# Another order of steps, weight loads and splits in a hybrid attention block on one Trainium2 core

## The chip, the cores and the metric

The kernel runs on one core of one Trainium2 chip, in one launch. The metric is device time in microseconds (us), lower is better; the inputs lie in HBM in a layout made ahead of the launch. The engines are TensorE (PE, matrix products; PEld is its weight load), VectorE (DVE), ScalarE (ACT), GpSimd (POOL) and SyncE (SP, which here issues nearly all DMAs). Each runs its own instructions in the order in which the program wrote them, and waits where one of them needs another engine's result.

## The reference

One block on `x` (512 tokens, width 1024): a norm, one wide input projection, four mixers of 512 columns each, an output projection with a residual, and a final norm. Float32 throughout.

```python
h = rmsnorm(x, norm_g)
p_fox, p_ssm, p_nsa, p_mem = split(h @ w_in)
mem_kv = rmsnorm(mem, mem_norm_g) @ w_mem_kv
# fox: 8 heads of 64: causal softmax attention, scores + c[q] - c[k] with c = cumsum(log_sigmoid(f + bias)); * silu(gate)
# ssm: causal conv of 4 taps, silu, state-space recurrence in chunks of 128, gated by silu(z), group norm
# nsa: 8 query heads on 2 key heads: attention to compressed blocks + chosen blocks + window, with a distance bias
#      (512 tokens: every block is chosen); three gates; * silu(gate)
# mem: 4 heads of 128, softmax attention to 256 memory tokens; * silu(gate)
x = x + concat(o_fox, o_ssm, o_nsa, o_mem) @ w_out
out = rmsnorm(x, final_norm_g)
```

## The kernel before

**Tiles and splits.** TensorE multiplies in a reduced form (`fp32r`). To hold float32 accuracy every operand is split in a rounded part and a remainder, and a product is three: high x high, low x high, high x low. The normed activations are `hh` and `hl` (high and low), eight 128x512 pieces of each. The weights come as 75 tiles of 128x1024 in one array, in the order of the table `ORDER`. A tile is named by what it projects and its number: `fq`, `fk`, `fg` are queries, keys and gate of fox; `xb`, `z` the convolution's input and the gate of ssm; `nq`, `ng`, `ks`, `kw`, `kc`, `vc` queries, gate, selected, window and compressed keys and values of nsa; `mq`, `mk`, `mv`, `mg` those of mem; `bv`, `bc` columns wanted first; `wo0` to `wo3` the output projection of the four mixers.

Each tile passes three steps. `load` issues its DMA on SyncE into one of three buffers `raw`. `split` rounds it on ScalarE to `wh` and subtracts, on VectorE or GpSimd, to `wl`; there are three buffers of `wh` and `wl` too, and a `raw` buffer is free after the subtraction. Then TensorE runs the tile's products: 24 of 128x512 into a PSUM tile `pj`, which other engines read off. What reads `pj` depends on the kind of tile: for `fq` into `L` and `M` (each with an upper and a lower half), for `fk` into `Rk` and `Rl`, for `kc`, `vc` into `kv` and on into `xst` and `xp`.

**Mixers.** Five pipes (fox, ssm, nsa, mem, cmp for the compression; a sixth prepares the distance bias) take their blocks through stages. In fox, stage 0 multiplies `L`, `M` with `Rk`, `Rl` into `pS`, takes the softmax (`pF`, with `nm` the negative maximum, `sm` the sum, `rs` its reciprocal), later stages transpose through DRAM (`fl` to `far` to `pt`, on SyncE's queue), and stage 3 multiplies with the values into `pO`. In ssm `m`, `ce`, `yc`, `xde`, `sq` are masks with exponentials, decayed inputs, outputs and squares; `rmr` is the mean-square root of the memory's norm. In nsa `ct` is a transposed tile of probabilities of the compressed blocks.

**What sets the order.** The engines' programs are written out by one pass over the string `PLAN`, two characters for each step. `L0` issues the next load, `W0` splits the next tile, `.n` runs n pieces of the projection in hand (a piece is three products, or the evacuation of the finished tile), a letter `f`, `s`, `n`, `m`, `c` or `p` with a digit runs that stage of that pipe for its next block, `O` splits the output of a mixer and `B` takes a step of the memory's norm. Since `PLAN` has `W` steps, the scheduler follows it strictly (`follow`), and a tile that is needed and not yet split is split then (`get`). The third table, `PICKS`, gives for each name of a tile a string of letters: which engine does the first, the second, the third copy or subtraction with this name (A ScalarE, V VectorE, P GpSimd). `pick` reads it. No timing model takes part in what follows the front of the program. The opening, up to the tile `fq0`, is written by code of its own.

All instructions are recorded by one helper, so that every row of the profile has its line, L360; tiles are told apart by name.

Of the kernel before, what the change touches and what calls it, by code (L numbers as in the profile page):

```python
# [16 lines left out]
S, D, M = 512, 1024, 256  # L17
# [34 lines left out]

ORDER = (
# [9 lines left out]
)  # L63
KEYS_A = [k for k in ORDER if k[0] not in ("bv", "bc", "mv") and k[0][:2] != "wo"]


PLAN = (
    "p0.9W0.8L0.5W0.2L0p1W0.7L0L0.2W0.9L0L0.6W0.6W0f0f0f0.6L0L0.3f1.6W0.1W0.5f0L0.4f1.6W0f1.3L0f1L0.6W0.3"
    "f2.5L0.1f3.1f0f2f0f0f2.3W0W0f2.4f3f1.2f1.4f2f2f4.5f3.1f3W0f0f4f0L0.6f4.2f5.1f1L0.3f3.1W0L0.4W0f4f1f0"
    "f2f0f1.6L0L0.5f3f3.6W0W0f0.2f1f1f2.1f2.2f4f4.1W0f3f3s0.1f4f1f4f0f0f0f1f1f1f4f2f2.2f3.5L0L0.4f5f2f2.1"  # L70
    "f2f3f2.4W0W0.6f4L0L0f0L0f3c0.1W0.3f5.1f3f5f5f5f3.5W0.9.1f4f4f5.4f4f4O0f1f5f5L0.1s0s0.3L0f2s1s1.5W0.2"
    "f5W0.2f5f5f3f3s2f5c1f4f5s3f4f5B0f5O0c2O0W0.1O0s1.9.3s0L0W0.3s2s2c3s3L0s3.2L0L0.5s4s1.9.2W0W0.3s2L0s5"
    "W0s3B0B0B0.2L0.3s4L0s4s4.1B0.1W0.9.6W0W0s5s5s5n0n0.7L0.2L0n1.3W0W0.2L0L0L0n0n1n0.1n1.3n2n2n2.8n1W0n3"
    "n0.1n1W0.5n2W0L0n3n4n4n2.4n0n0n3n5n5n3L0.8n1n1W0L0n4n0.2O1O1.2n2.3n3.3n2.2W0.1n3n0.1n0n0n1n1.3O1.3L0"
    ".1L0.3n2W0W0n5.2n1n1n0n0n4n4n4.4L0.1n2W0O1.7n1n1n3n4n2n2n3n3n2n0L0.2n3n3n0n5.5W0n5n3n2.4L0.1n5n3n0n4"
    "n4.1n5n5.4n0n1n4n4n0L0n1n1W0n2n0n2n4.3n1.1n2.3n5L0.4W0.3n5.4n2W0n5n5.3n1n1n3n0n0n0.8L0L0.1n3W0n2n1n1"
    ".4n3n3n3.3n1n4n4n4n4.1W0n5n2W0n5n5n5n0n0n0n0.3n1.1n4.1n2n2.1n2.2L0n3.3W0.9n3.1n1n3.2B0n4n4.2n0L0L0n2"
    ".3L0n4.1n4n1W0n1n2n5n5n3.1W0.2n5.3n0n0n3n1n3.8n2.1n0.3n0W0L0L0n2.5n2n1n5n1n4n4n4n3n1W0n3n3n0n2.2n2n1"
    "n4n4.1n3.3n4W0.9n2.3L0m0m0L0m0.2W0L0.3W0.2n1m1n5m1n5n5n5n4m1n2.2n5n5O2n5n3n3m2.1n2W0.4m2.1m3.1m2.1m3"
    "m3m4n4m0m0m0m0n5m4m4n3n5.1n3.1m5m5O2m1m1n4.1n4m2L0n4n5n5m2L0m1m3m6n5L0m2m5O2O2m3m3m0.2m4.1W0.4m4.5W0"  # L80
    "m4.3m5m5m5m1m1m2W0m6m6m2m3m3.1L0.1L0.3m4m4L0.2m6.4W0.4m6m6.1m5m5.1W0.2m6m6.2W0.9.9.9.9.1"
)


PICKS = {
    "M": "VAAAVVVA",
    "Rk": "AVVAAVVV",
    "Rl": "VAAAAAVA",
    "ce": "PPVVVV",
    "ct": "AVAAVAVVAAVAVVVA",  # L90
    "kh0": "AVV",
    "kh1": "AVV",
    "ll": "PVPVPPVV",
    "m": "PVVPVPVV",
    "ml": "PVPV",
    "ol": "VVPVPPVPVPPVPPV",
    "pF": "VVVVVVVAVAVVVVAVAAVVVVVAAVVVAVVV",
    "pM": "VAAVVVAAVAVVVAVA",
    "pN": "AVVVAAVVAVAAAAVAVAVAVAAAVVVVVAAVAAVAVVAAAVVVAVAVAAAVAVVAVVAAVVVV",
    "sq": "VPVPVPPV",  # L100
    "wl": "PVPPPPPPPPPPVVVPVPVPPVVVPPPVPPVVPVVPVPPVPVPPVVPVPPVPPPPVVPPPPPVPVPVPPPVV",
    "xde": "VVV",
    "xp": "VVPVVVVV",
    "yc": "PVVVVVVVVVVPVVVP",
}


# [2044 lines left out]
```

## Time and profile before

| | |
|---|---|
| time, median of 3 runs | 511.45 us (511.14 to 514.05) |
| the profiled execution | 511.3 us, its span 509.5 us, mean granted clock 0.997 |
| busy in the span: PE, DVE, ACT, POOL | 97%, 72%, 58%, 32% |
| weight tiles loaded / split | 75 of 512 KB each |
| bytes moved by DMA | 92.66 MB, mean 182 GB/s |

TensorE is busy nearly all the time and is what the other engines feed. "Busy" counts a row from its start to its modelled end, and rows of TensorE overlap, so a gap shown is a little shorter than the time lost. "Idle before, releaser" in the profile names what ended a wait. The front of the program, to about 42 us, loads and projects `bv` and `bc`; then come fox with the first tiles of ssm and of the compression (to about 180 us), ssm with the output projection of fox (to about 260), nsa (to about 440) and mem with the last tiles of the output projection.

### The profile page before, as it was taken

The page shows a single profiled execution, that of the slowest core. Times are in us where ns is not written, and L with a number is a line of the kernel's source. Part 1 is how long each engine was busy: PE and PEld are TensorE (multiplying, and loading weights), DVE is VectorE, ACT ScalarE, POOL GpSimd, SP SyncE. Part 2 cuts the span into 40 slices and gives each one's busy share as a digit, 9 for nine tenths or more (in the row PEclk, how much of TensorE's full clock was granted, in tenths as well). Part 3 has the DMA queues.
Part 4 walks back from the last instruction along what each step waited for, and adds up shares of the span by engine and source line. Part 5 has one row for each costly group of instructions (what it writes and reads, how often), then busy time and mean ns, then how long its engine had stood idle before and what let it go on. Part 6 is the DMA issues. An engine that isn't in the chain of part 4 may idle for free.

```text
span 509.5 us, 8995 instructions
## 1 busy us (share of the span) xinstructions
PE 496.4 (97%) x2965; PEld 419.6 (82%) x2965; DVE 368.9 (72%) x981; ACT 297.3 (58%) x671; POOL 164.4 (32%) x113
## 2 busy tenths in 40 slices
PE   8999999989999999999899999999999999999995
PEld 5898877877788888888788888788888898898884
DVE  5486686667678688997988786787777786655644
ACT  5856366777545535664464776755756654664343
POOL 3594303030133103643653132340251220521532
PEclk9999999999999999999999999999999999999998
DMA  8791824526687679444345477777766776832213
GB/s 300 314 326 53 93 85 144 183 79 170 155 262 214 194 228 373 130 171 170 132 152 172 123 225 198 238 219 213 197 196 212 233 233 163 255 138 83 84 41 124
DMA packets 72446, 92.66 MB, mean 182 GB/s; under 512 B 26784, under 2 KB 50624, under 8 KB 72400
## 3 DMA queue, kind: packets, MB, share of 16 engines
q1 hardware_dynamic: 71968, 91.51, 58.5%
q10 hardware_dynamic: 432, 0.59, 0.3%
q8 instruction: 23, 0.38, 0.3%
q14 instruction: 23, 0.19, 0.1%
HBM read 73.68 MB, written 20.55 MB: 185 GB/s over the span
## 4 chain that ended last, share of the span: by engine, by line
PE 56%; DVE 19%; ACT 9%; DMA 6%; issue 5%; SPq 2%; POOL 2%; POOLq 0%; ACTq 0%; DVEq 0%
PE pj L360 25%; PE po L360 10%; PE pb L360 7%; PE pO L360 5%; PE pS L360 4%; ACT pN L360 3%; DMA raw<-in_wst 3%; DVE wl L360 2%; DVE fl L360 2%; SPq L360 2%; DVE pN L360 1%; DVE xs L360 1%; ACT pF L360 1%; DMA far<-fl 1%; DVE rs L360 1%
## 5 line engine op out<-in xcount | busy, mean ns | idle before, releaser
L360 POOL TENSOR_TENSOR wl<-raw,wh 128x1024 fp32r<-128x1024 f32 (+1 forms) x44 | 109.3, 2493 | 258.9 <-ACT wh L360 182.9
L360 PE MATMUL pj<-hh,wl 128*128 128x512 f32 x352 | 137.6, 391 | 3.5 <-POOL wl L360 2.8
L360 PE MATMUL pj<-hh,wh 128*128 128x512 f32 x352 | 138.5, 393 | 0.5 <-ACT wh L360 0.5
L360 PE MATMUL pj<-hl,wh 128*128 128x512 f32 x352 | 137.2, 390 | 0.0
L360 PEld LDWEIGHTS pj<-hh,wl 128*128 128x128 f32 x352 | 66.1, 188 | 19.1 <-POOL wl L360 3.6
L360 ACT ACTIVATE wh<-raw 128x1024 fp32r<-128x1024 f32 (+1 forms) x72 | 73.3, 1034 | 8.5 <-DMA raw<-in_wst 3.4
L360 PEld LDWEIGHTS pj<-hh,wh 128*128 128x128 f32 x352 | 66.1, 188 | 14.7 <-ACT wh L360 0.9
L360 PEld LDWEIGHTS pj<-hl,wh 128*128 128x128 f32 x352 | 66.1, 188 | 13.0
L360 ACT ACTIVATE pN<-pN,nm 128x128 f32<-128x128 f32 (+7 forms) x96 | 45.3, 473 | 37.5 <-DVE nm L360 36.3
L360 DVE TENSOR_TENSOR wl<-raw,wh 128x1024 fp32r<-128x1024 f32 (+1 forms) x29 | 37.8, 1310 | 4.6 <-ACT wh L360 4.1
L360 PE MATMUL po<-wh,oh 128*128 128x512 f32 x96 | 37.7, 393 | 0.0
L360 PE MATMUL po<-wh,ol 128*128 128x512 f32 x96 | 37.5, 390 | 0.0
L360 PE MATMUL po<-wl,oh 128*128 128x512 f32 x96 | 37.5, 390 | 0.0
L360 ACT ACTIVATE pF<-pF,nm 128x128 f32<-128x128 f32 (+3 forms) x32 | 17.8, 556 | 28.3 <-DVE nm L360 27.4
L360 DVE TENSOR_TENSOR acc<-acc,po 128x512 f32<-128x512 f32 (+1 forms) x33 | 21.1, 663 | 9.9 <-PE po L360 9.8
L360 DVE STREAM_TRANSPOSE fl<-pN 128x128 f32<-128x128 f32 (+3 forms) x64 | 27.9, 482 | 0.1
L360 DVE SCALAR_TENSOR_TENSOR rs<-sm,gat 128x3 f32<-128x3 f32 x32 | 6.6, 206 | 28.8 <-ACT pN L360 28.8
L360 ACT ACTIVATE pN<-pN,rs 128x128 f32<-128x128 f32 (+3 forms) x31 | 16.1, 544 | 12.9 <-DVE rs L360 12.9
L360 DVE CUSTOM_DVE_ANT_0 pN<-pS,bt 128x128 f32<-128x128 f32 (+5 forms) x80 | 22.1, 320 | 0.1
L360 DVE SCALAR_TENSOR_TENSOR xs<-x,cwh,xs 128x512 f32<-128x512 f32 x24 | 19.0, 790 | 4.0 <-ACT xs L360 3.4
L360 PEld LDWEIGHTS po<-wh,ol 128*128 128x128 f32 x96 | 18.0, 188 | 3.8
L360 PEld LDWEIGHTS po<-wl,oh 128*128 128x128 f32 x96 | 18.0, 188 | 3.6
(273 smaller groups left out, 1009.2 us busy)
## 6 DMA issues: line engine op xcount, KB each, us to landing
raw<-in_wst SPq DMA_DIRECT2D x73, 512.0 KB, 5.0
far<-fl SPq DMA_DIRECT2D x144, 64.0 KB, 2.1
pt<-far SPq DMA_DIRECT2D x36, 256.0 KB, 3.9
far<-fl SPq DMA_DIRECT2D x96, 48.0 KB, 1.7
pt<-far SPq DMA_DIRECT2D x24, 192.0 KB, 2.9
rows<-rv SPq DMA_DIRECT2D x4, 656.0 KB, 7.1
bt<-rows SPq DMA_DIRECT2D x4, 528.0 KB, 4.9
xn<-in_xn SPq DMA_DIRECT2D x4, 512.0 KB, 7.2
```

The source lines that it names most:

```text
L360: return f(*a, **k)
```

## The change

`ORDER`, `PLAN` and `PICKS` are replaced by others; nothing else is. Pools, stages, the number of buffers and the arithmetic of every step are the same.

```diff
 ORDER = (
     ("bv", 0), ("bv", 1), ("bv", 2), ("bv", 3), ("bc", 0), ("bc", 1), ("bc", 2), ("fq", 0), ("xb", 6),
-    ("fk", 1), ("xb", 3), ("xb", 0), ("fk", 0), ("kc", 0), ("fk", 3), ("fk", 2), ("fq", 1), ("fq", 3),
-    ("fq", 2), ("fg", 0), ("vc", 0), ("xb", 1), ("z", 2), ("xb", 5), ("fg", 2), ("z", 3), ("xb", 7), ("fg", 3),
+    ("fk", 1), ("xb", 3), ("xb", 0), ("fk", 0), ("kc", 0), ("fk", 3), ("fq", 2), ("fq", 1), ("fq", 3),
+    ("fg", 0), ("vc", 0), ("xb", 1), ("fk", 2), ("xb", 5), ("fg", 3), ("z", 2), ("fg", 2), ("xb", 7),
...
-    ("ks", 0), ("nq", 2), ("mv", 0), ("mv", 1), ("mv", 2), ("mv", 3), ("nq", 1), ("mg", 3), ("wo0", 2),
...
+    ("wo0", 1), ("nq", 2), ("ks", 0), ("mv", 0), ("mv", 1), ("mv", 2), ("mv", 3), ("nq", 1), ("mg", 3),
...
 PLAN = (
-    "p0.9W0.8L0.5W0.2L0p1W0.7L0L0.2W0.9L0L0.6W0.6W0f0f0f0.6L0L0.3f1.6W0.1W0.5f0L0.4f1.6W0f1.3L0f1L0.6W0.3"
...
+    "L0L0.9.1W0.1p0.5W0.4L0.4L0.5W0.2L0.9W0.5W0.9p1f0f0.5L0.9W0W0L0f1.4W0.7L0L0.5f1f0.3W0.1f0f1f1.2L0f2.1"
...
 PICKS = {
-    "Rk": "AVVAAVVV",
-    "Rl": "VAAAAAVA",
+    "Rk": "VVAAAAAV",
+    "Rl": "VAAVVVAA",
...
-    "pF": "VVVVVVVAVAVVVVAVAAVVVVVAAVVVAVVV",
+    "pF": "AAVAVVVAAAVVVVVVAAVAVVAAVAAAAVVA",
...
-    "wl": "PVPPPPPPPPPPVVVPVPVPPVVVPPPVPPVVPVVPVPPVPVPPVVPVPPVPPPPVVPPPPPVPVPVPPPVV",
+    "wl": "PVPPPPPPPPPPPPVPPVPVPVVPPPPVPPVPPVPVPVVPPVPPVPVPPPPPPPPPPVPPPPVPPPVVPPVP",
...
```

`PLAN` has 690 steps instead of 694: as many loads but one (63), as many splits (64) and stages, and the same pieces of projection (582) in 171 steps instead of 175. In `PICKS`, GpSimd subtracts 52 weight remainders of 72 instead of 44; ScalarE scales 16 of 32 fox probabilities (`pF`) instead of 8; five `Rk` copies instead of three and four `Rl` copies instead of six are ScalarE's; three of the `xp` sums more and one `xde` are GpSimd's. The front of each engine's program and its end stay as they were.

Three places follow, as the engines' programs have them, one row for each instruction or run of like instructions: operation, what is written, what is read, the size. First ScalarE in the fox stretch, before the change. The first `wh` is the split of `fq3`, the second that of `fq2`, the `L` and `M` rows read off `fq1`, and the last `wh` is the split of the gate tile `fg0`.

```order
L360 CAST Rk<-pj 64x512
L360 ACTIVATE wh<-raw 128x1024
L360 ACTIVATE Rk<-pj 64x512 x2
L360 CAST Rl<-cr 64x512
L360 ACTIVATE wh<-raw 128x1024
L360 ACTIVATE pF,sm<-pF,nm 128x512 x2
L360 ACTIVATE pF<-pF,rs 128x512
L360 ACTIVATE L<-pj 64x512 x2
L360 CAST M<-L 64x512
L360 ACTIVATE M<-cst 64x512
L360 CAST M<-L 64x512
L360 ACTIVATE wh<-raw 128x1024
```

The same place after the change; the first row of `wh` are the splits of `fq1` and `fq3`, the first `L` and `M` rows read off `fq2`, and the single `wh` is that of `fg0`.

```order
L360 ACTIVATE Rk<-pj 64x512 x2
L360 CAST Rk<-pj 64x512 x2
L360 ACTIVATE wh<-raw 128x1024 x2
L360 ACTIVATE L<-pj 64x512 x2
L360 ACTIVATE M<-cst 64x512
L360 CAST M<-L 64x512
L360 ACTIVATE M<-cst 64x512
L360 ACTIVATE wh<-raw 128x1024
L360 ACTIVATE L<-pj 64x512 x2
L360 CAST M<-L 64x512
```

The three query tiles ahead of `fg0` are `fq1`, `fq3`, `fq2` before and `fq2`, `fq1`, `fq3` after; in both its split follows the evacuation of the first of them. Before, the softmax rows of 512 (`pF`) stand ahead of that evacuation, after they don't, and more attention products lie between the split and its use. The evacuation of the key tile `fk2` (the second group of `Rk`) has left this place.

Second GpSimd, as a difference, from the root of the memory's norm (`rmr`) to the compression's sums (`xp`).

```order
 L360 TENSOR_TENSOR wl<-raw,wh 128x1024
 L360 TENSOR_TENSOR rmr<-rmv,nhalf 128x2
-L360 TENSOR_TENSOR wl<-raw,wh 128x1024 x11
+L360 TENSOR_TENSOR wl<-raw,wh 128x1024 x16
 L360 MEMSET xp 128x16x2
 L360 TENSOR_TENSOR xp<-xst,x_89 128x8x31
 L360 MEMSET xp 128x16x2
+L360 TENSOR_TENSOR xp<-xst,x_89 128x8x31 x3
```

Five more subtractions stand in this run, and three more sums come behind it.

Third ScalarE in the ssm stretch, ahead of nsa's first query tiles. Before, where the three `wh` are `ks0`, `nq2` and `mv0`:

```order
L360 ACTIVATE sq<-yc 128x512 x2
L360 ACTIVATE L<-pj 64x512 x2
L360 ACTIVATE ce<-m 128x512 x2
L360 ACTIVATE m<-m,nacs 128x128 x8
L360 ACTIVATE wh<-raw 128x1024 x3
L360 ACTIVATE sq<-yc 128x512
```

After, where they are `nq2`, `ks0` and `mv0`:

```order
L360 ACTIVATE sq<-yc 128x512
L360 ACTIVATE ce<-m 128x512 x2
L360 ACTIVATE m<-m,nacs 128x128 x8
L360 ACTIVATE L<-pj 64x512 x2
L360 ACTIVATE wh<-raw 128x1024 x3
L360 ACTIVATE sq<-yc 128x512 x2
```

The exponentials of the ssm chunk (`ce`, `m`) have moved ahead of the evacuation `L` of the query tile before; the three splits stand behind both as before, and more of TensorE's work lies between the first of them and its use.

More of the change, by code (lines that the diff above doesn't have):

```diff
@@ L67 @@
 PLAN = (
-    "p0.9W0.8L0.5W0.2L0p1W0.7L0L0.2W0.9L0L0.6W0.6W0f0f0f0.6L0L0.3f1.6W0.1W0.5f0L0.4f1.6W0f1.3L0f1L0.6W0.3"
[L69 to L81, printed above, removed]
+    "L0L0.9.1W0.1p0.5W0.4L0.4L0.5W0.2L0.9W0.5W0.9p1f0f0.5L0.9W0W0L0f1.4W0.7L0L0.5f1f0.3W0.1f0f1f1.2L0f2.1"
@@ new lines @@
+    "L0.1W0.9.2f0f2f2f0f2.3W0W0.3L0f0.7f1f1L0f1.6W0f3.2f3.2L0.3f4W0f2f4.1f0f1.5W0.3f3f3f3f2f2f3.8f0f0L0f0"
+    "L0L0.2f2.1f3.6f1.4W0.4L0f1.1f1W0W0f2f0s0f3f3.2f4f0f0f4f4f4f1f4f2f2f2f4f0f1f1f1.4f4.1W0f3.1L0.5L0.2W0"
+    "f3f0.2L0f2f3f2f5.5f3f4f4B0f1f5f5f5f5.1W0.1f5.6L0.8c0s0W0f4f5.9.2f2f5W0f5f2f5s1s1f5f3f5.5f4f4L0L0W0.1"
+    "f3.3f5.1f3L0W0s2c1s3L0O0s0f4f4c2f5f5f5s1.9s0.5O0O0O0.2s2W0s2c3s3s1s4L0.9s2W0.7L0L0.3s5.1W0W0s3s3B0B0"
+    ".1B0.4B0.2s4s4s4.9W0.1L0.6L0.2s5s5W0W0s5n0L0n0L0.6W0.5W0n1n0n1L0n0n1.1L0.2L0.1n2n2.2W0n2.5W0.3n1n0n1"
@@ new lines @@
+    ".1L0.7n3n3W0L0.1n2n0n4n0n3n2.4n3.1L0.2n4O1.2n1n1W0n0n5.4O1O1.4n4.3W0.2n1n2n3n3W0n0n0n0.9.1L0.2n2W0n1"
+    "n2n1n1n3n4n4L0n4n0n0n4n2n2.3n3.5n2n3n3O1.4n5n5n5W0.1n1n1L0n0n0.4n3.1W0n5n5.3L0L0.1n2n2n0n3W0n4n4.1L0"
+    ".6n1n1n1n2n3n0n0n0.9W0.2n2n5.2n1n1n1n4L0n4n4n2n5n5.2n0n3W0n0.2L0.6n2.3n3.4W0.1n0n1.1n2n3.1W0.4L0W0n4"
+    "n4n4n4n1n3n5n2n5L0n1n2n2n0n5n0.1n0n0n4.2n5n2n1.1n5.1n5.1n3n3n3n3.9n5W0.1n4n5.2n1.2L0.4L0n4.4n1n4n1.4"
+    "W0W0n0n2n0n0.6n3n3L0n2n1.1n2.2n3n4B0.4n1n3.3n0.1n2L0W0.2n0n2n2.2n4n4n4n1n4n5n1W0n0.3n3n3.2n1L0L0.5n3"
@@ L82 @@
+    ".7W0.1m0n4m0m0n5n5n5n4n4W0.1n2n2n2.6n1n5m1m1m2m3L0L0n5n5n5m1.3W0.3n3.1n5.1n5.1m2m2W0.1m0m4m3m5O2n5m3"
+    "m4m4m0m0m5m0m5n2.1n3n3n3.2m1m1n4n4n5n4n4n5n5n5O2O2L0O2W0m2m1m1m0.2m2m2m3m3m2.2m4m4.1m3.5L0L0L0m4.2W0"
+    "m1W0W0m3L0L0m5m5m2.2m3.1m6.1m6.3m6.1m6.3W0.1m4.1W0.2m4.5m5m5m6m6m5m6m6.9.9.9.9.5"
 )
 PICKS = {
-    "M": "VAAAVVVA",
-    "Rk": "AVVAAVVV",
-    "Rl": "VAAAAAVA",
[L89 to L94, printed above, removed]
@@ L95 @@
-    "ml": "PVPV",
-    "ol": "VVPVPPVPVPPVPPV",
-    "pF": "VVVVVVVAVAVVVVAVAAVVVVVAAVVVAVVV",
-    "pM": "VAAVVVAAVAVVVAVA",
-    "pN": "AVVVAAVVAVAAAAVAVAVAVAAAVVVVVAAVAAVAVVAAAVVVAVAVAAAVAVVAVVAAVVVV",
-    "sq": "VPVPVPPV",
-    "wl": "PVPPPPPPPPPPVVVPVPVPPVVVPPPVPPVVPVVPVPPVPVPPVVPVPPVPPPPVVPPPPPVPVPVPPPVV",
-    "xde": "VVV",
-    "xp": "VVPVVVVV",
-    "yc": "PVVVVVVVVVVPVVVP",
+    "M": "VAVAAAVA",
+    "Rk": "VVAAAAAV",
+    "Rl": "VAAVVVAA",
+    "ce": "PPPVVV",
+    "ct": "AAAAVVAAAAAVVAAA",
@@ L105 @@
+    "kh0": "VVV",
+    "kh1": "VVV",
+    "ll": "PVPVPVVP",
+    "m": "VVVPPVVV",
+    "ml": "PVPP",
+    "ol": "VVPPPPVPPVVPVVV",
+    "pF": "AAVAVVVAAAVVVVVVAAVAVVAAVAAAAVVA",
+    "pM": "AVVAAAAVAAVAVVVV",
+    "pN": "AVVVVAVVVAAAAAVAVVAAVVVVAAVAAAAVVAVAAAVVVAAVAVAVVVAVAVVVVAVVVVVV",
+    "sq": "PVVVPPVV",
+    "wl": "PVPPPPPPPPPPPPVPPVPVPVVPPPPVPPVPPVPVPVVPPVPPVPVPPPPPPPPPPVPPPPVPPPVVPPVP",
+    "xde": "PVV",
+    "xp": "PVVVVPPP",
+    "yc": "VVPVVPPPVVVVPVVV",
 }
```

10 rows, old and new, of the table ORDER are left out of this document.

## The prediction

> **What bounds the kernel now.** I read the page's first part, then the stretches, then TensorE's table of waits, then single places in the timeline.
>
> ```profile
> PE 496.4 (97%) x2965; PEld 419.6 (82%) x2965; DVE 368.9 (72%) x981; ACT 297.3 (58%) x671; POOL 164.4 (32%) x113
> ```
>
> TensorE is busy for 496.4 of 509.5 us. The change takes no matrix product away, so all it can win is the 13.1 us in which TensorE stands still. The columns of the next view are the stretch, its length, then for each engine its busy time and instructions, the granted clock, the DMA share and GB/s.
>
> ```profile
> 0.00:42.00 42.00, 40.36 (x210) 33.48 (x211) 22.97 (x32) 26.58 (x41) 27.08 (x19) 1.00 0.81 295
> 42.00:130.00 88.00, 84.94 (x385) 69.43 (x384) 65.74 (x157) 57.03 (x110) 16.81 (x9) 1.00 0.46 116
> 130.00:232.00 102.00, 102.00 (x683) 86.19 (x683) 81.65 (x166) 54.69 (x118) 30.58 (x20) 1.00 0.67 212
> 232.00:310.00 78.00, 76.72 (x423) 64.55 (x419) 62.92 (x195) 46.81 (x108) 32.48 (x25) 1.00 0.55 169
> 310.00:425.00 115.00, 114.08 (x789) 98.21 (x788) 88.66 (x345) 72.28 (x204) 32.08 (x25) 1.00 0.72 211
> 425.00:509.50 84.50, 78.27 (x489) 67.70 (x487) 46.92 (x90) 39.91 (x95) 25.40 (x18) 0.98 0.40 130
> ```
>
> Length less busy PE gives the idle time: 1.64, 3.06, 0, 1.28, 0.92 and 6.23 us. The first and the last stay: the opening loads and the final sums and stores keep their order. What can go is 3.06 + 1.28 + 0.92 = 5.26 us, 1% of the time. The granted clock is 1.00 until the last stretch, so no slower TensorE hides in these rows. The second stretch, where the fox heads' tiles are projected, waits most.
>
> ```profile
> PE pj L360 <- POOL wl L360: 2.8, 2, 1.5
> PE pO L360 <- ACT ct L360: 0.8, 1, 0.8
> PE pj L360 <- DVE wl L360: 0.5, 1, 0.5
> PE pj L360 <- ACT wh L360: 0.5, 1, 0.5
> PE pS L360 <- DVE Rl L360: 0.4, 1, 0.4
> ```
>
> These are TensorE's waits: what waited, for whom, us in total, times, the longest. Four of them, 4.2 us, are for a query or key matrix or the two halves `wh`, `wl` of a weight tile. Such waits depend on how far ahead a split stands in the order, which is what the change rewrites.
>
> **How a wait is priced.** A projection of a tile is a run of 512-wide `pj` products. A row of the chain of waits shows their pace:
>
> ```profile
> 148.49 10.24 PE pj L360 x45
> ```
>
> That is 0.228 us each, though a single row lasts 0.39 us since neighbours overlap. A wait costs what start to start exceeds 0.228, about 0.16 us more than the idle time shown. A tile of 24 such products takes 5.46 us.
>
> **The gate tile `fg0`, 112.59 us.**
>
> ```profile
> 104.90 0.72 ACT L360 ACTIVATE pF<-pF,nm 128x512 f32<-128x512 f32 x1 [4.07 <-DVE nm L360]
> 107.40 1.21 ACT L360 ACTIVATE L<-pj 64x512 fp32r<-64x512 f32 x2
> 108.64 0.62 ACT L360 CAST M<-L 64x512 fp32r<-64x512 f32 x1
> 110.95 1.04 ACT L360 ACTIVATE wh<-raw 128x1024 fp32r<-128x1024 f32 x1
> 112.07 2.37 POOL L360 TENSOR_TENSOR wl<-raw,wh 128x1024 fp32r<-128x1024 f32 x1 [8.54 <-ACT wh L360]
> 112.59 0.39 PE L360 MATMUL pj<-hl,wh 128*128 128x512 f32 x1
> 114.50 0.50 PE L360 MATMUL pj<-hh,wl 128*128 128x512 f32 x1 [1.52 <-POOL wl L360]
> ```
>
> The tile's `wh` is queued on ScalarE behind a softmax row that waited 4.07 us for a maximum and behind the evacuation of the query tile `fq1` (107.40 to 110.95). Its `wl` then ran on GpSimd until 114.44. TensorE paid 114.50 − 112.59 − 0.23 = 1.68 us. In the new order no softmax row stands between the evacuation of the keys and this `wh`; two whole tiles (10.9 us) and some attention products lie between it and its use, where before it was some 7.5 us, and its `wl` is on VectorE. Evacuation, copy and subtraction take 3.55 + 1.04 + 2.37 = 6.96 us even on GpSimd; that leaves 3.9 us to spare. **−1.68.** A softmax row as late as before would eat those 3.9 us; it stands behind this `wh` now.
>
> **The tile `xb1`, 126.49 us.**
>
> ```profile
> 126.25 2.00 ACT L360 ACTIVATE wh<-raw 128x1024 fp32r<-128x1024 f32 x2
> 126.49 0.39 PE L360 MATMUL pj<-hh,wl 128*128 128x512 f32 x1
> 127.35 0.50 PE L360 MATMUL pj<-hh,wh 128*128 128x512 f32 x1 [0.47 <-ACT wh L360]
> 127.69 0.40 PE L360 MATMUL pj<-hl,wh 128*128 128x512 f32 x1
> 128.61 0.50 PE L360 MATMUL pj<-hh,wl 128*128 128x512 f32 x1 [0.53 <-DVE wl L360]
> ```
>
> Two gaps: 0.86 − 0.23 = 0.63 and 0.92 − 0.23 = 0.69, 1.32 us. Counting the products that stand between a split and its first use, this split moves from about 6.1 to 9.8 us ahead. The 3.7 us are more than the 1.32 missing. **−1.32.**
>
> **The keys at 82 us.** TensorE waited 0.4 us for `Rl`. More of the `Rk` copies are on ScalarE in the new tables and more of the `Rl` on VectorE; the chain is as long, some half a microsecond further ahead. I take half: **−0.2**, between 0 and −0.4.
>
> **The first selected-key tile, 247.92 us.**
>
> ```profile
> 243.50 2.45 ACT L360 ACTIVATE m<-m,nacs 128x128 f32<-128x128 f32 x8 [1.19 <-DVE m L360]
> 245.85 3.09 ACT L360 ACTIVATE wh<-raw 128x1024 fp32r<-128x1024 f32 x3
> 246.97 5.88 POOL L360 TENSOR_TENSOR wl<-raw,wh 128x1024 fp32r<-128x1024 f32 x2 [2.95 <-ACT wh L360]
> 247.92 0.39 PE L360 MATMUL pj<-hl,wh 128*128 128x512 f32 x1
> 249.59 0.51 PE L360 MATMUL pj<-hh,wl 128*128 128x512 f32 x1 [1.28 <-POOL wl L360]
> ```
>
> 1.67 − 0.23 = 1.44 us. Three splits were asked for at once behind eight exponentials. In the new order the tile used first here (`nq2`) is split some 11 us of TensorE's work ahead, and its subtraction is on VectorE. **−1.44.** The eight exponentials still stand ahead of it; they would have to come 7 us late to bring the wait back.
>
> **What is late next.** With these waits gone, the next to be late is a split with a short lead. The tightest I find is `fq1`: two splits stand behind four `Rk` copies of the key tile `fk3`, with one tile between.
>
> ```profile
> L360 ACT ACTIVATE Rk<-pj 64x512 fp32r<-64x512 f32 x8 | 4.7, 584 | 0.1
> L360 DVE TENSOR_TENSOR wl<-raw,wh 128x1024 fp32r<-128x1024 f32 x27 | 36.4, 1357 | 4.6 <-ACT wh L360 4.1
> L360 POOL TENSOR_TENSOR wl<-raw,wh 128x1024 fp32r<-128x1024 f32 x42 | 106.2, 2538 | 250.7 <-ACT wh L360 174.6 <-PE pO L360 24.1 <-DVE ql L360 16.8
> ```
>
> Four `Rk` (2.34), one VectorE subtraction between them (an estimate of 0.7 for 64x512 from the 1.357 of a 128x1024 one), `wh` (1.04) and `wl` (1.36) are 5.4 us; TensorE needs `wl` after 5.46 + 0.46. The slack is half a microsecond. Other places have splits 1 to 3 us ahead, as before had. Nothing shows what they will cost: at least 0 (the stretch from 130 to 232 us has none over 683 products), at most the 5.26 us of before. I take **+0.92**, the idle time of the stretch from 310 to 425, the nearest row of a stretch with short leads and no single long wait.
>
> **Who does what.** Of 72 subtractions 52 instead of 44 are on GpSimd: 8 × 1.36 = 10.9 us off VectorE and 8 × 2.54 = 20.3 us onto GpSimd, which is busy for 32%. Eight more softmax scalings go to ScalarE (58% busy):
>
> ```profile
> L360 ACT ACTIVATE pF<-pF,rs 128x512 f32<-128x512 f32 x3 | 2.2, 725 | 0.7 <-DVE rs L360 0.7
> ```
>
> at most 8 × 0.73 = 5.8 us. TensorE works beside all of this, so I cost it at nothing; without that cover a `wl` on GpSimd is 1.18 us later for its tile than on VectorE, and a row on ScalarE up to 0.73 us. TensorE's own instructions are the same and the pieces of projection are too: 0.
>
> **Queues.** A weight load moves with its split, on SyncE's queue, past stores and reads of the softmax tiles.
>
> ```profile
> L360 ACT ACTIVATE wh<-raw 128x1024 fp32r<-128x1024 f32 (+1 forms) x72 | 73.3, 1034 | 8.5 <-DMA raw<-in_wst 3.4
> raw<-in_wst SPq DMA_DIRECT2D x73, 512.0 KB, 5.0
> far<-fl SPq DMA_DIRECT2D x144, 64.0 KB, 2.1
> ```
>
> ScalarE waited 3.4 us in all for a landing, and no wait of TensorE's that I list is for one. A load that falls behind a store landing after 2.1 us is that much later against three buffers of lead. I take 0, with bounds 0 and +3.4. On GpSimd's queue `xp` and `xde` of the ssm stretch come in behind the splits; that stretch has no idle time on TensorE, so 0, bounded by one split, +2.54.
>
> **The sum.** From the profiled execution's 511.3 us (its span 509.5; 0.15 under the median): 511.3 − 1.68 − 1.32 − 0.2 − 1.44 + 0.92 = **507.6 us**.
>
> **GpSimd beside VectorE.** Here a row speaks against the change.
>
> ```profile
> 50.81 4.94 POOL L360 TENSOR_TENSOR wl<-raw,wh 128x1024 fp32r<-128x1024 f32 x2
> 51.49 2.00 DVE L360 CAST M<-L 64x512 fp32r<-64x512 f32 x1
> 119.41 0.42 DVE L360 CAST M<-L 64x512 fp32r<-64x512 f32 x1
> ```
>
> The same cast takes 0.42 us alone and 2.00 us beside GpSimd's subtractions: 1.58 us for one meeting. A split moved to GpSimd frees 1.36 us of VectorE, so from 0.86 meetings per moved split on, VectorE loses.
>
> The Trainium skill, page "SBUF — State Buffer", section "SBUF: two separate sides", states that VectorE and GpSimd share one port pair, which is an exclusive lock and not a split of the bandwidth: whichever starts first keeps it for its whole instruction, and the other fully blocks. This trace agrees, with 2.00 against 0.42 us. By that rule the eight moved splits could each stop VectorE for as long as they last, and the result would be the third rival's below.
>
> **The rivals.**
>
> *A. All the waits go.* For it: the stretch from 130 to 232 us shows that a long run without idle time is possible, and the order there is of the same kind. Against: the short leads named above. 511.3 − 5.26 − 8 × 0.16 (what the overlap of rows hides of some eight waits) = 504.7 us.
>
> *B. The change doesn't do what it says.* The waits go from these four places and as many open elsewhere, since ScalarE's and VectorE's work is the same in sum and a split can only be early if something else is late: 511.3 us. For it: `fq1`'s half microsecond. Against: ScalarE idles for 42%, so earlier splits push out little.
>
> *C. Slower, by meetings of VectorE and GpSimd in the fox and early ssm stretch.* The run of splits on GpSimd between `rmr` and `xp` grows from 11 to 16. Two meetings for each of the five added cost 5 × (2 × 1.58 − 1.36) = 9.0 us of VectorE. Half of it on the path of the softmax and of the evacuations, with no wait gone, gives 511.3 + 4.5 = 515.8 us; how much reaches TensorE no row shows (0 to 9.0). It decides from 0.86 meetings per moved split. For it: VectorE is busy for 65.74 of 88 us there. Against: GpSimd is busy for 16.81 of these 88, and only casts and copies are shown stretched.
>
> **How the numbers follow.** My forecast, 505.5 to 509.7 us, gets 0.47; A 0.20; B 0.20; C 0.13. The range, 504.0 to 515.0, reaches over A and B and into C; what lies outside is most of C's upper half and a little under A, some 0.1 to 0.2. A measurement tells about 1% from no change here, 506.3 and 516.6 us. Below 506.3 lie A and a quarter of the forecast's own range: 0.32. Above 516.6 lies half of C: 0.07. The rest is 0.61.
>
> **What would show it.** Right: the stretch of 42 to 130 us has about 1 us of idle TensorE instead of 3.06, that of 232 to 310 under 0.5; the table of waits has no 1.5 us wait of `pj` for GpSimd's `wl`; GpSimd's group of `wl` counts 50 instead of 42. Wrong: a new TensorE wait of over 1 us for `wl`, `wh`, `L` or `Rk`, `fq1`'s near 92 us above all (B); VectorE casts of 2 us in number beside GpSimd's splits and a longer busy VectorE although it has fewer instructions (C); ScalarE's wait for landings above 3.4 us (the queue). The forecast fails most easily in the +0.92, which no row of before fixes.

## The result and the profile after

The changed kernel takes **505.38 us** (median of 4 runs, 505.26 to 505.7) against 511.75 us before in the same comparison (511.14 to 514.05): a ratio of 0.9869, 95% interval 0.9843 to 0.9896. That is 6.4 us or 1.3% less, where the prediction's sum took off 3.7 us; the time lies between the forecast (507.6) and rival A (504.7), just under the forecast's own 505.5 to 509.7 us. The profiled execution took 505.46 us with a span of 503.7, so span against span 5.8 us went.

The stretches of the changed kernel, columns as before (stretch, length, busy time of PE, PEld, DVE, ACT, POOL, granted clock, DMA share, GB/s):

```profile
0.00:42.00 42.00, 40.40 (x209) 33.26 (x210) 22.87 (x31) 26.24 (x40) 26.76 (x19) 1.00 0.81 293
42.00:130.00 88.00, 86.70 (x397) 71.53 (x397) 61.66 (x150) 56.70 (x112) 24.17 (x11) 1.00 0.51 131
130.00:232.00 102.00, 102.00 (x690) 86.85 (x689) 77.03 (x166) 59.42 (x128) 39.98 (x27) 1.00 0.70 226
232.00:310.00 78.00, 78.00 (x421) 66.02 (x420) 62.23 (x194) 49.34 (x112) 37.00 (x29) 1.00 0.50 151
310.00:425.00 115.00, 115.00 (x827) 99.96 (x825) 82.94 (x337) 71.29 (x199) 32.94 (x26) 1.00 0.73 213
425.00:503.70 78.70, 72.44 (x432) 62.54 (x430) 45.70 (x85) 38.34 (x91) 23.45 (x16) 0.98 0.35 121
```

From 130 to 425 us TensorE has no idle time left. Of the 5.26 us that could go, 1.30 are still there, all in the fox stretch. TensorE's waits, the whole table:

```profile
PE pw L360 <- DVE warm L360: 1.3, 1, 1.3
PE pj L360 <- POOL wl L360: 1.3, 1, 1.3
PE pb L360 <- DVE fv L360: 0.3, 1, 0.3
```

The first and the third belong to the opening; the second is one wait, at 65 us, for the split of the tile `xb0`. The share of the chain that ended last, by engine, says the same: TensorE carried 56% of it before, with 19% VectorE and 9% ScalarE, and now

```profile
PE 92%; DMA 2%; DVE 2%; ACT 2%; issue 1%; POOL 1%; POOLq 0%; ACTq 0%
```

**Where the 5.83 us come from.** I compared, over all 2965 TensorE rows of both traces, the distance from each start to the next with the median distance, in both traces together, after a row of the same names and sizes. What is more than 0.15 us over the median sums to 7.74 us before and 2.97 after: 4.77 us are long waits. All smaller deviations, above and below the median, sum to 7.69 and 6.63: 1.06 us. At the four places of the prediction 5.36 us were lost before (0.92 at 82 us, 1.68, 1.32, 1.44) and none is lost there now. The tile `fg0`, which cost the most, is split in time:

```profile
100.94 1.04 ACT L360 ACTIVATE wh<-raw 128x1024 fp32r<-128x1024 f32 x1
102.01 1.23 DVE L360 TENSOR_TENSOR wl<-raw,wh 128x1024 fp32r<-128x1024 f32 x1 [0.93 <-ACT wh L360]
104.65 0.40 PE L360 MATMUL pj<-hl,wh 128*128 128x512 f32 x1
104.89 0.39 PE L360 MATMUL pj<-hh,wl 128*128 128x512 f32 x1
```

The remainder is ready at 103.24, TensorE reads it at 104.89, 0.24 us after its neighbour.

**The one wait left.** Rows of the timeline around 65 us:

```profile
51.22 0.38 SPq L360 DMA_DIRECT2D rmd<-rmr  x1
51.71 15.64 SPq L360 DMA_DIRECT2D raw<-in_wst  x4
63.49 1.06 ACT L360 ACTIVATE wh<-raw 128x1024 fp32r<-128x1024 f32 x1 [2.01 <-DMA raw<-in_wst]
64.62 2.37 POOL L360 TENSOR_TENSOR wl<-raw,wh 128x1024 fp32r<-128x1024 f32 x1 [8.53 <-ACT wh L360]
65.37 0.39 PE L360 MATMUL pj<-hl,wh 128*128 128x512 f32 x1
67.05 0.50 PE L360 MATMUL pj<-hh,wl 128*128 128x512 f32 x1 [1.29 <-POOL wl L360]
```

SyncE's queue holds a small store (`rmd` from `rmr`, the memory's norm) until GpSimd has the value at 51.2 us. Four weight loads stand behind it, ScalarE waits for the first of them until 63.5, and the subtraction, now on GpSimd instead of VectorE, ends 1.46 us late (67.05 − 65.37 less the usual 0.226, before rounding). The kernel before had the same late loads (10.4 us to landing), but this subtraction on VectorE, and lost nothing here.

### The profile page after: what moved, and what is told of

It is laid out like the page before. It is cut to its first block, busy times and chain, and to the rows that moved or that the text cites. A ratio compares the mean times of both kernels' runs of the same rounds, so it can differ in the third digit from the quotient of the medians.

```text
span 503.7 us, 8985 instructions
## 1 busy us (share of the span) xinstructions
PE 494.5 (98%) x2965; PEld 420.1 (83%) x2965; DVE 352.4 (70%) x960; ACT 301.3 (60%) x679; POOL 184.3 (37%) x126
## 4 chain that ended last, share of the span: by engine, by line
PE 92%; DMA 2%; DVE 2%; ACT 2%; issue 1%; POOL 1%; POOLq 0%; ACTq 0%
PE pj L360 46%; PE po L360 17%; PE pO L360 7%; PE pb L360 6%; PE pS L360 6%; DMA raw<-in_wst 2%; PE pmv L360 2%; PE pW L360 1%; PE pY L360 1%; PE pT L360 1%; PE pcm L360 1%; PE pw L360 1%; ACT wh L360 1%; DVE hl L360 1%; PE pst L360 1%
## 5 line engine op out<-in xcount | busy, mean ns | idle before, releaser
L360 POOL TENSOR_TENSOR wl<-raw,wh 128x1024 fp32r<-128x1024 f32 (+1 forms) x52 | 125.8, 2426 | 228.0 <-ACT wh L360 223.6
L360 PEld LDWEIGHTS pj<-hh,wh 128*128 128x128 f32 x352 | 66.1, 188 | 13.6 <-issue 0.7
L360 DVE TENSOR_TENSOR wl<-raw,wh 128x1024 fp32r<-128x1024 f32 (+1 forms) x21 | 25.3, 1206 | 4.2 <-ACT wh L360 4.1
L360 ACT ACTIVATE pN<-pN,rs 128x384 f32<-128x384 f32 (+3 forms) x27 | 15.2, 582 | 10.7 <-DVE rs L360 10.7
L360 PEld LDWEIGHTS po<-wh,oh 128*128 128x128 f32 x96 | 18.0, 188 | 3.7 <-issue 0.2
```

The lines of the kernel that those rows point to most:

```text
L360: return f(*a, **k)
```

## The experiments

At the start I held that the *order* won: splits stand earlier, so the waits go, and the table of engines (`PICKS`) is nearly free. The rivals were *load* (VectorE has less to do) and *fit* (the tables are good only together). All times are given with their ratio to the kernel before in the same call, since that one moved between 511.75 and 512.73 us; the changed kernel's is 0.987.

### The two halves of the change

The tables swapped whole: once `ORDER` and `PLAN` as before with `PICKS` as after, once the other way round.

```diff
 # old order, new picks            # new order, old picks
-PICKS = {before}                  -PICKS = {after}
+PICKS = {after}                   +PICKS = {before}
```

> Order of tiles and steps as before, engines of the copies and subtractions as after. Theory 'order' (the four waits went because the splits are asked for earlier): the picks alone win little, 510 to 513 us, and the waits for wl or wh near 112, 126 and 247 us are still there in some form. Rival 'load' (the gain is VectorE's 17 us of work less): 506 to 508 us, idle TensorE between 42 and 425 us under 2 us. Rival 'fit' (each table of picks only suits its own order): 513 us or more, with new waits.

> Order of tiles and steps as after, engines as before. Theory 'order': 505 to 508 us, nearly the whole gain. Rival 'load': 510 to 512 us. Rival 'fit': above 511 us, with waits that neither of the two kernels shows.

Measured: old order with new engines **525.72 us**, ratio 1.0265 (1.025 to 1.028); new order with old engines **522.82 us**, 1.0209 (1.0189 to 1.0229). Each half alone makes the kernel slower, by 13.6 and 10.7 us, though both together win 6.4. *Order* falls and *fit* stands; *load* is not tested by the first run, as the busy times below show. The longest waits of the two without that of the opening, first of the old order with new engines, then of the new order with old engines:

```profile
PE pj L360 <- DVE wl L360: 3.9, 2, 3.4
PE pst L360 <- ACT m L360: 2.2, 1, 2.2
PE pY L360 <- DVE prev L360: 2.2, 1, 2.2
PE pW L360 <- DVE sg L360: 1.5, 1, 1.5
```

```profile
PE pj L360 <- DVE wl L360: 2.2, 3, 0.9
PE pS L360 <- DVE sg L360: 2.0, 2, 1.4
PE pn L360 <- DVE prev L360: 1.3, 1, 1.3
PE pj L360 <- POOL wl L360: 1.1, 2, 0.8
```

By length some two thirds of the waits behind the opening are for VectorE. Many are for tiles that neither kernel waits for, but the longest, 3.4 us in the first run, is for `ks0`, for which the kernel before waits too.

The two halves lose in different ways. In the new order with old engines VectorE is busy for 370.9 us with as many rows as before (981; 368.9 there). The subtraction of `xb0`, on VectorE again, waits 3.08 us at the head of the queue for its `wh`, with ready rows behind it; what that costs is measured below with this one letter moved. In the old order with new engines VectorE has the 960 rows of the changed kernel, which take 352.4 us there, and needs 368.4: 16 us are rows that last longer beside GpSimd, the kind of loss that rival C forecast. Two of them, then GpSimd beside the second and TensorE behind it:

```profile
225.04 5.13 DVE L360 TENSOR_TENSOR xde<-xdt,dte 128x512 f32<-128x512 f32 x1
254.15 2.94 DVE L360 TENSOR_TENSOR wl<-raw,wh 128x1024 fp32r<-128x1024 f32 x1
253.66 5.66 POOL L360 TENSOR_TENSOR wl<-raw,wh 128x1024 fp32r<-128x1024 f32 x2 [3.90 <-ACT wh L360]
257.15 0.49 PE L360 MATMUL pj<-hh,wl 128*128 128x512 f32 x1 [3.36 <-DVE wl L360]
```

In the changed kernel such an `xde` takes 1.07 us on average and such a `wl` 1.26. The first row ends at 230.17 and TensorE's 2.2 us wait at 230.32, with a product that reads this `xde` (the table puts it down to `m`); the second row ends just ahead of the 3.4 us wait's end.

A part of both losses is TensorE's own clock. Their traces have stretches of 3.41 us in which it was granted at half speed, two in the first (at 230 and 258 us) and one in the second (at 262 us). `pj` products then start every 0.43 us instead of 0.23, and each stretch costs TensorE 1.6 to 1.8 us. The first run's stretch from 232 us on, with a clock of 0.97:

```profile
232.00:310.00 78.00, 72.06 (x411) 60.47 (x411) 60.72 (x177) 40.19 (x93) 28.33 (x24) 0.97 0.47 146
```

Neither the kernel before nor the changed one has such a stretch before TensorE's last products. Each of the three came within 0.6 us of the end of a TensorE wait of 1.1 to 3.5 us, but other waits as long (1.9 us at `fq1` with all subtractions on GpSimd) brought none; what sets it off is not shown.

### Which engines matter

The changed kernel with one string put back, `wl` (44 subtractions on GpSimd, on other tiles), and with all strings but `wl` put back.

```diff
-    "wl": "PVPPPPPPPPPPPPVPPVPVPVVPPPPVPPVPPVPVPVVPPVPPVPVPPPPPPPPPPVPPPPVPPPVVPPVP",
+    "wl": "PVPPPPPPPPPPVVVPVPVPPVVVPPPVPPVVPVVPVPPVPVPPVVPVPPVPPPPVVPPPPPVPVPVPPPVV",
```

> The changed kernel with one string of the engines put back: the weight remainders as before (44 and not 52 on GpSimd, and on other tiles); all other strings as after. If the weight remainders carry the fit of the two tables, most of the 17 us between the changed kernel and its order with the old engines comes back: 515 to 523 us. If the many small strings (pF, pN, Rk, ct and so on) carry it: 505.5 to 509 us.

> Order as after, the weight remainders' engines as after, all other strings as before. With the old string of remainders alone the changed kernel took 513.4 us, with all old strings 522.8. If the parts add, this is 505.4 + 9.4 = 515 us. If each old string spoils the rest, it is nearer 520; if only the remainders mattered with the others beside them, 506 to 509 us.

Measured: old `wl` alone **513.38 us**, 0.9997 (0.9971 to 1.0023); the others old **510.88 us**, 0.998 (0.997 to 0.999). Against 0.987 the first costs 1.3% (6.6 us), the second 1.1% (5.7 us), both together 3.4% (17.4 us): more than their sum, so each spoils the other's fit. Each lies between its readings: the first is not most of the loss and more than a little, the second is below the 515 us that adding would have given, since the 17.4 us hold an interplay of some 5 us (1.7 of it, in the profiled execution, the half-clock stretch with all old strings).

All 72 subtractions on GpSimd:

```diff
-    "wl": "PVPPPPPPPPPPPPVPPVPVPVVPPPPVPPVPPVPVPVVPPVPPVPVPPPPPPPPPPVPPPPVPPPVVPPVP",
+    "wl": "PPPPPPPPPPPPPPPPPPPPPPPPPPPPPPPPPPPPPPPPPPPPPPPPPPPPPPPPPPPPPPPPPPPPPPPP",
```

> The changed kernel with every weight remainder on GpSimd (72 of 72). VectorE is freed of 20 more subtractions (24 us), GpSimd gets 48 us. If VectorE's queue is the scarce thing and GpSimd's length costs nothing, 504 to 506 us, with waits for GpSimd's wl alone. If splits close together wait for each other on GpSimd (2.4 us each) or meet VectorE's copies there, 508 to 520 us.

Measured **511.7 us**, 0.9977 (0.9956 to 0.9998): 5.5 us slower than the changed kernel, inside the second reading. VectorE lost 20 rows of 1.2 us, 24 us, but its busy time fell only from 352.4 to 341.1: some 13 us came back, most of it as rows that last longer beside GpSimd, about 0.6 us for each moved split. TensorE's waits are for GpSimd:

```profile
PE pj L360 <- POOL wl L360: 3.5, 3, 1.7
PE pmv L360 <- POOL wl L360: 1.5, 1, 1.5
```

Unloading VectorE onto GpSimd does not pay by itself.

### One subtraction moved

On the kernel before, `fg0` and `ks0` to VectorE; on the changed one, `xb0`.

```diff
-    "wl": "PVPPPPPPPPPPVVVPVPVPP...   (before: letters 20 and 38, counted from 0)
+    "wl": "PVPPPPPPPPPPVVVPVPVPV...   (both V)
...
-    "wl": "PVPPPPPPPPPPPPVPP...       (changed kernel: letter 12)
+    "wl": "PVPPPPPPPPPPVPVPP...
```

> The kernel before, but the weight remainders of fg0 and ks0, for which TensorE waited 1.68 and 1.44 us on GpSimd, are subtracted on VectorE. If the wait is that of one slow subtraction, each falls by about 1.2 us: 509 us. If VectorE's queue is what is short there, as the run with xb0 on VectorE showed, the time stays or grows, with new waits for VectorE behind: 511 to 515 us.

> The changed kernel, but the weight remainder of the tile xb0 is subtracted on VectorE (as it was before) and not on GpSimd. The one long wait left, 1.46 us at 65.4 us, should shrink by what VectorE is faster, about 1.2 us: 504.2 us. If VectorE is busy with other work there, or the wait moves to the next tile (fk0), no gain: 505.4 us.

Measured: **518.09 us**, 1.0094 (1.0062 to 1.0126), and **507.58 us**, 0.9914 (0.9898 to 0.993): slower by some 5 and 2.2 us, both outside their readings. In the first the wait of `fg0` did fall from 1.68 to 0.49 us, as one faster subtraction should make it. That of `ks0` did not: 1.54 us from start to start instead of 1.44, now for VectorE, where the subtraction follows two sums of the output. Others opened, led by 2.31 us at 126 us for a `wh` (it had been 0.63):

```profile
PE pj L360 <- DVE wl L360: 2.6, 4, 1.4
PE pW L360 <- DVE sg L360: 2.2, 1, 2.2
PE pj L360 <- ACT wh L360: 2.1, 1, 2.1
PE pn L360 <- POOL sq L360: 1.5, 1, 1.5
```

Two half-clock stretches (at 130 and 263 us) add 3.2 us in this trace, a good part of what was lost.

The second run shows how one subtraction can delay others. VectorE at 62 us, in the changed kernel and, behind it, with `xb0` on VectorE:

```profile
62.23 0.19 DVE L360 TENSOR_SCALAR nacs<-pa 128x32 f32<-128x32 f32 x1
62.68 0.42 DVE L360 CAST Rl<-cr 64x512 fp32r<-64x512 f32 x1
65.87 0.68 DVE L360 CAST Rk<-pj 64x512 fp32r<-64x512 f32 x1 [2.76 <-ACT Rk L360]
```

```profile
64.87 1.23 DVE L360 TENSOR_TENSOR wl<-raw,wh 128x1024 fp32r<-128x1024 f32 x1 [2.73 <-ACT wh L360]
66.13 0.19 DVE L360 TENSOR_SCALAR nacs<-pa 128x32 f32<-128x32 f32 x1
66.57 0.42 DVE L360 CAST Rl<-cr 64x512 fp32r<-64x512 f32 x1
68.00 0.68 DVE L360 CAST Rk<-pj 64x512 fp32r<-64x512 f32 x1 [1.01 <-ACT Rk L360]
```

The subtraction waits at the head of the queue for its late `wh`, and the ready work behind it waits too: `nacs` starts 3.9 us later, `Rk` 2.13 us later. From there VectorE and ScalarE hand each other the convolution's and the keys' evacuations with no slack that takes it up: the same 2.13 us are still there at 94.59 and 96.72, where the remainder of `fq1` is subtracted. TensorE won 0.85 us at `xb0` and lost 2.7 us at six places up to 98 us.

### The store ahead of the loads

The store of the memory's norm is issued behind the load of tile 14 and not where the norm is worked out. On the changed kernel this puts it behind four more loads:

```diff
     r = rsq(ms, 2, 1.0 / D, "rm")
-    Q.dma_start(out=rmd.rearrange("t p -> p t"), in_=r)
+    state["rmd"] = r
...
         Q.dma_start(out=raw[i], in_=I["wst"][i])
     state["load"] += 1
+    if i == 14:
+        Q.dma_start(out=rmd.rearrange("t p -> p t"), in_=state["rmd"])
```

> The changed kernel, but the store of the memory's norm (rmd from rmr) stands on SyncE's queue behind the next four weight loads and not ahead of them. In the changed kernel that store waited for GpSimd until 51.2 us and four loads stood behind it; the load of xb0 landed 11.7 us after its issue, and ScalarE waited for it until 63.5. If the queue behind the store sets the wait at 65.4 us, the loads start 3 to 7 us earlier and the wait goes: 503.9 us. If the landing is slow for another reason (all loads share the DMA engines), the wait stays: 505.4 us.

> The store behind four weight loads on the changed kernel, once more, beside the other runs of this call: 503.3 to 504.2 us, and no TensorE wait over 0.15 us between 42 and 425 us.

Measured **503.66 us**, 0.984 (0.9824 to 0.9856), and once more 503.87 us, 0.984 (0.9824 to 0.9856): 1.7 and 1.5 us below the changed kernel, by the ratios 1.5 us both times, the fastest version here. No wait of TensorE's is left between 42 and 425 us, and TensorE is 96% of the chain that ended last. Its fox stretch, with as much TensorE work as time:

```profile
42.00:130.00 88.00, 88.00 (x405) 73.08 (x404) 63.76 (x154) 58.20 (x114) 24.25 (x12) 1.00 0.50 134
```

The loads had two reasons to be late. They were issued from 51.71 us on; with the store moved three of the four are issued between 43.4 and 56.3 us and the store at 65.19. The next rows show the second: ten microseconds of the changed kernel, the store's own row, and the same ten microseconds with the store moved. The store is 1 KB, written element by element across partitions.

```profile
50.00:60.00 10.00, 10.00 (x50) 8.38 (x49) 8.30 (x22) 4.08 (x9) 5.61 (x3) 1.00 0.90 24
rmd<-rmr SPq DMA_DIRECT2D x1, 1.0 KB, 8.5
```

```profile
50.00:60.00 10.00, 10.00 (x49) 8.38 (x49) 8.27 (x23) 3.98 (x9) 5.60 (x3) 1.00 0.33 105
```

The store takes 8.5 us to land, and while it does the DMA engines are busy for 90% of the time and move 24 GB/s; the loads behind it landed 10.4 us after their issue. Moved, the share is 33% at 105 GB/s, and loads there land after 3.3 us; the store, which takes 9.8 us in its new place, holds up no load there that TensorE waits for. The packets of the changed kernel's trace say what fills the 90%. The store's pieces of 4 bytes start between 52.11 and 52.36 us and show 7 to 9 ns each. Sixteen packets of 4096 bytes follow from 52.74 us on and take 3.1 to 8.8 us each, where one takes 0.16 us from 62 us on. It is packets of the loads that stand in the engines; what holds them there is not shown. The Trainium skill, page "DMA: Bandwidth & Descriptors", section "Two DMAs through the same engine are not ordered", states that within one queue of one DMA engine descriptors start in order. These starts agree: all of the store's come ahead of the first load's.

The same edit on the kernel before:

> The kernel before, with the store of the memory's norm behind four weight loads, as in the run on the changed kernel. There it took 1.7 us away. If the late loads reach TensorE in the kernel before too, by way of the keys' split at 82 us and the late queue of ScalarE, it gains 1 to 2.5 us: 509.5 to 511 us. If its own waits at 112, 127 and 248 us hide the early loads, no change: 511.7 us.

Measured **516.42 us**, 1.005 (1.0019 to 1.0082): neither reading; it is slower, with a new TensorE wait of 1.23 us at 101.5 us and the wait of `fg0` grown to 0.62 + 1.87. Loads that come early are no gain where something else sets the pace. The trace does not explain the median: it took 513.68 us, with a mean granted clock of 0.996 and no half-clock stretch ahead of the end. In eight of the ten executions the clock was 0.990 to 0.995, in half of those of the kernel before at least 0.997. A lower clock goes with the loss; what lowered it no trace shows.

Both single edits together, the store moved and `xb0` on VectorE:

> Both single edits: the store behind four weight loads, and the remainder of xb0 on VectorE. On the changed kernel alone the latter cost 2.2 us, because the subtraction waited 2.7 us for its wh at the head of VectorE's queue with ready work behind it. With the load early its wh is early: if the head of the queue was the cause, the time is that of the store's edit, 503.7 us, within 0.5; if VectorE's 1.2 us of work is the cause, it is 505 to 506 us.

Measured **505.04 us**, 0.9863 (0.9847 to 0.9879), 1.2 us above the store's edit alone in the same call (503.87). Here `wh` is early and the subtraction waits only 0.26 us at the head of the queue, and the second reading holds: its own 1.23 us matter as well. Nothing between 62 us and `fq1` takes the delay up. It shows at `fq1`, VectorE with the store moved, then VectorE and TensorE with both:

```profile
92.70 1.22 DVE L360 TENSOR_TENSOR wl<-raw,wh 128x1024 fp32r<-128x1024 f32 x1 [0.27 <-ACT wh L360]
```

```profile
94.50 1.23 DVE L360 TENSOR_TENSOR wl<-raw,wh 128x1024 fp32r<-128x1024 f32 x1 [0.27 <-ACT wh L360]
93.80 0.39 PE L360 MATMUL pj<-hh,wl 128*128 128x512 f32 x1
94.52 0.50 PE L360 MATMUL pj<-hh,wh 128*128 128x512 f32 x1 [0.33 <-ACT wh L360]
94.86 0.39 PE L360 MATMUL pj<-hl,wh 128*128 128x512 f32 x1
95.78 0.50 PE L360 MATMUL pj<-hh,wl 128*128 128x512 f32 x1 [0.53 <-DVE wl L360]
```

1.80 us later on VectorE cost TensorE 0.49 + 0.69 = 1.18 us: the slack at `fq1` was 0.6 us.

### The lead of one split

The split of `fg0` is moved behind seven more pieces of projection, and with them behind the evacuation of `fq1`.

```diff
-    "...f1.4W0.7L0L0.5f1f0.3W0.1..."
+    "...f1.4.7W0L0L0.5f1f0.3W0.1..."
```

> The changed kernel, but the split of fg0 stands behind one more evacuation (that of fq1), some 7.0 us of TensorE's work ahead of its use instead of 11.8; before the change it was 7.5. If the lead alone made the wait of 1.68 us, it comes back: 507 us. If it was the late queue of ScalarE (softmax rows that waited 4.07 us for VectorE ahead of the split), evacuation, copy and subtraction take 3.65 + 1.05 + 1.26 = 6.0 us, inside 7.0, and the time stays at 505.4 us.

Measured **507.02 us**, 0.9903 (0.9886 to 0.992), 1.6 us above the changed kernel; the number suits the first reading, the trace does not. TensorE has no wait at `fg0`. Its waits behind the opening (the line is L347, since `PLAN` takes fewer lines there):

```profile
PE pj L347 <- POOL wl L347: 1.7, 1, 1.7
PE pj L347 <- DVE wl L347: 0.2, 1, 0.2
```

The first is that of `xb0` at 65 us again, 1.87 us from start to start instead of 1.46, ahead of the place of the edit; small ones at 156 and 166 us (0.35 and 0.22) are new. So a lead of 7.0 us is enough for `fg0` when ScalarE's queue is on time and the subtraction is on VectorE, as it is in the changed kernel. On GpSimd, as before the change, evacuation, copy and subtraction would take some 7.1 us (an estimate from 3.65 + 1.05 + 2.37), so this run does not say that the 7.5 us of the kernel before were ample. The 0.41 us at 65 us and the rest of the 1.6 stay unexplained; one profile can't tell them from the spread of landings.

## Why the prediction was right, and where it was wrong

**What bounds the kernel**: right. TensorE's idle time was all there was to win, and 3.96 of the 5.26 us in the three middle stretches went.

**The four places**: all four waits went, −5.36 us from start to start where I put −4.64. The place mis-sized is 82 us: I priced it from the table of waits (0.4 us) and took half; from start to start it was 0.92 us in two steps, and it went whole. For the three others the sizes are those forecast. For `fg0` three reasons were given. The longer lead was not needed: the run with a lead of 7.0 us had no wait there. The subtraction on VectorE is worth 1.19 of the 1.68 us by the run that moved it in the kernel before. Softmax rows that wait for VectorE ahead of the split are left for the other 0.49, though no run put those rows back by themselves. For `ks0` the engine alone, in the kernel before, did nothing, so there the place in the order counts.

**The small waits that I kept** (`ct` at 319 us and others, 1.59 us): I left them in without a term, and 0.34 us remains. Together with TensorE's small steps, forecast at 0 and measured at −1.06 us, this is why the time fell further than forecast.

**The new waits, +0.92**: one of 1.46 us came, not at `fq1` but at `xb0`. Its two causes stood in the text with their prices and were both set to nothing: a remainder on GpSimd is 1.18 us later for its tile, and a load falls behind a store. I had looked at the queue for stores that land after 2.1 us; the one that counted waits for GpSimd and takes 8.5 us. So it is luck that the +0.92 was near a wait that came: it was taken for splits with a short lead. `fq1`'s slack, estimated at half a microsecond, is 0.6 us by the run with both edits. Six of the kernels tried lost time there, and with the store moved it is the tightest place found in the fox stretch. Two of the prediction's signs of being wrong did show: a new wait of over 1 us for a `wl`, and ScalarE's wait for landings, 7.8 us instead of 3.4.

By these sizes the sum is −5.36 − 1.25 + 1.46 − 1.06 + 0.4 (the opening, 0.78 before, 1.18 after) = −5.8 us, the difference of the spans.

**Who does what, at nothing**: the step that failed in its reasoning. I took idle shares (ScalarE 42%, GpSimd 68%) as cover for moved copies. Put back, the old engines cost 17.4 us, and a single subtraction on the other engine 1.2 to 2.2 us. An idle share was no cover: what mattered was whether ready work stood behind a waiting row (2.73 us at the head of VectorE's queue) and whether a row met GpSimd.

**Rivals.** A had nearly the right time: the measured 505.46 of the profiled execution is 0.8 us above it. B (waits only move) fell for the change; each half of the change alone did worse than that. C (VectorE and GpSimd meet more often) fell for the change, but not for its tables of engines in the old order. Single rows do meet, as this one of the kernel with the store moved (0.42 us in the changed kernel):

```profile
62.56 2.51 DVE L360 CAST Rl<-cr 64x512 fp32r<-64x512 f32 x1
```

In the changed kernel VectorE's busy time fell from 368.9 to 352.4 us, and with all subtractions on GpSimd a moved split brought back about 0.6 us of its 1.2; there the point from which VectorE loses was not reached. In the old order the same table left 368.4 us: what the moved rows freed came back whole, and TensorE lost time behind it. A meeting can cost more than the 1.58 us of the prediction (4.1 us for the `xde` above), and how many there are depends on the order.

## What to carry to other kernels

In a kernel whose bound engine is 97% busy, a wait is not a local price: the engines that feed it hand work to each other in order, and one row that waits at the head of a queue moves everything behind it by as much, to surface at the next tight place 30 us on. And the same table of engines lets VectorE's rows meet GpSimd's or pass them, by the order: 16 us of VectorE's time here. So a table of order and a table of engines are to be changed together, and half of a good change can be slower than none. When one wait is left, follow it through the queues back to a transfer: the last 1.5 us here were a 1 KB store that stood ahead of the weight loads.

## What the runs showed of the hardware

A store of 1 KB that writes element by element took 8.3 to 9.8 us to land. Beside it the DMA engines were busy for 90% of their time with 24 GB/s, as 4096-byte packets of the loads behind it took up to 8.8 us instead of 0.16; half-megabyte loads behind it landed after 10.4 us, with the store moved after 3.3.

VectorE's rows lasted longer only beside GpSimd, and only where they touch SBUF tiles alone. Counted over all 14 traces, 343 of the 1058 such rows that overlap a GpSimd row by over 0.3 us were more than 0.15 us longer than the quickest fifth of their form. Of 1533 such rows with a PSUM tile none was, and no row was that ran without a GpSimd row beside it.

TensorE's clock was granted at half speed for 3.41 us at a time in the middle of three of the slower kernels, at a cost of some 1.6 to 1.8 us each.
